# A decoder mixer layer on one core: weight-block sums moved and spread, linear attention's sums on another engine, and an extra turn for background steps

## The chip, the cores and the metric

The kernel runs on one core of a Trainium2 chip. The time is the device time of one execution in microseconds, as the median of several runs. In the profile PE is TensorE (PEld its weight loads), DVE is VectorE, ACT is ScalarE, POOL is GpSimd and SP is SyncE, whose queue here issues loads.

## The reference

One layer, 256 tokens, width 2048, all in float32. Two causal token mixers run side by side on one projection, are gated, merged and projected out:

```python
h = rmsnorm(x, pre_norm_g[l])
proj = h @ w_in[l]
(a_q, a_k, a_v, a_g, a_lr, b_q, b_k, b_v, b_g, m_a, m_b) = jnp.split(proj, offsets, axis=-1)
gk = jax.nn.log_sigmoid((a_lr @ gla_gk_w2[l] + gla_gk_b[l])) / GATE_LOGIT_NORMALIZER
o_a = gla_chunked(a_q, a_k, a_v, gk)            # 4 heads, keys 256, values 512, chunks of 64
o_a = rmsnorm(o_a, gla_norm_g[l]) * jax.nn.silu(a_g)
y_a = o_a @ w_branch_a[l]
o_b = diff_attention(b_q, b_k, b_v, lam)        # 16 heads, two softmaxes of 64 each, values 128
o_b = rmsnorm(o_b, diff_norm_g[l]) * (1.0 - lam_init) * jax.nn.silu(b_g)
y_b = o_b @ w_branch_b[l]
merged = jax.nn.sigmoid(m_a) * y_a + jax.nn.sigmoid(m_b) * y_b
x = x + rmsnorm(merged @ w_out[l], post_norm_g[l])
```

In `gla_chunked` the score of a query t and a key s is the sum over the key's elements of q, k and exp(b_t - b_s), where b is the running sum of the gate; in `diff_attention` the weights are one softmax minus lam times another.

## The kernel before

**Weights.** All weight matrices lie in one DRAM array in the order in which they are used. They are taken in halves of 128 x 1024 elements. `emit_half` loads a half (SP's queue), makes a rounded part `hi` of it on ScalarE (L244) and the rest `lo` on VectorE (L245); each product is then three matmuls: hi with both parts of the other operand, lo with the first part. `take` keeps four halves emitted ahead of the one in use (`AHEAD`); `hi` and `lo` have three buffers each. A token-major half (`half_tile`, L421) is 12 matmuls of up to 512 columns, a channel-major half (`half_channel`, L441 and L443) 8 of 512 and 8 of 256.

**Sets.** Five "sets" of weight blocks are multiplied by seven products instead of eight (`block_products`, L706), in the order 1, 3, 5, 6, 2, 7, 4. Each product has a left operand that is a sum of blocks. Per set and block row t = 0, 1 there are two running tiles, `a` and `b`, and a raw block. Product 1 takes `a`; then a DMA on POOL's queue adds a further block to `a` (L201). Product 3 takes `b`, product 5 takes `a`, product 6 takes a + b, product 2 the raw block, product 7 takes `b` after another accumulating DMA, and product 4 takes `a` plus the raw block. `emit_set` is called when a half is emitted, ahead of its split, and `follow_set` just behind the split. Products 1, 6, 7 and 4 accumulate in one PSUM bank `x`; between them VectorE or ScalarE reads it (L711, L717, L724). The set halves (six matmuls each) alternate with halves of other projections by the fixed order of `phase_steps`.

**Background work.** After the sets come token-major and channel-major projections: `ag0` to `ag3`, `m01`, the heads of groups 0 and 1, `m02`, `y00` to `y03` (branch a), the heads of groups 2 and 3, `m03`, `y10` to `y13` (branch b) and `o0` to `o3`. Under them run generators in the list `tasks`: `forget_gate`, `gla_scores` (one for each half of the four linear-attention heads), `gla_out`, and `diff_pair` (one for each two heads of a group of four). `pump(n)` gives one turn to each of the first n tasks: it runs them to their next `yield`. In token-major products it comes after every second half (after every half until the gate is done), in channel-major products after both halves of a channel. A task that yields after its last step is taken off the list by one more turn. A `diff_pair` makes for each of its two heads: scores (L933, L934) with the softmax's exponentials (L944), the combination (L951), transposes (L955), values (L963 to L965) with the norm (L969 to L976), and at the end transposes of both heads (L981). A group's pairs start when both pairs of the group before are done. `settle`, called in `y10` ahead of half 6, runs all tasks to their end.

**Linear attention's scores.** `gla_scores` fetches q and k from DRAM by POOL's queue, multiplies them on POOL (L769), adds channel pairs on POOL (L767), and in the first of seven levels does the same with a product shifted by one token (L785, L767). The results are split (L787 on ScalarE, L788 on VectorE).

**Order.** Instructions are listed in program order and then ordered for each engine by a planner with its own estimates of cost; an instruction may be placed earlier than its turn when its inputs and buffers are there. `issue_after` keeps TensorE's part of a turn behind the half last multiplied. Each engine runs its queue in that order and stands still at an instruction whose inputs are missing.

Of the kernel before, what the change touches and what calls it, by code (L numbers as in the profile page):

```python
# [91 lines left out]
def hybrid_kernel(ctx: ExitStack, tc, xt, xn, preg, postg, w, w2, gkb, glag, lamv, diffg, ident_d, causal_d, lmask_d, out):  # L92
# [84 lines left out]
    def emit_set(s, prod, t, h):  # L177
        c = slice(1024 * h, 1024 * h + 1024)
        if h == 0 and prod == 1:
            if s == 0:  # L180
                link(s, "a", t)
            link(s, "b", t)
        if h == 0 and prod == 4 and s + 1 < SETS:
            link(s + 1, "a", t)
        n = 4 * PRODUCTS.index(prod) + 2 * t + h + LEAD - 4 * PRODUCTS.index(2)
        if 0 <= n < 4:
            i, j = n // 2, n % 2
            raws[s, i, j] = u([P, 1024], "c")
            sp.dma_start(raws[s, i, j], weights(f"set{s}", 4 + i)[0][:, 1024 * j : 1024 * j + 1024])
        a, b = chain[s, "a", t], chain[s, "b", t]  # L190
        if prod == 6:
            dve.tensor_tensor(out=a[:, c], in0=a[:, c], in1=b[:, c], op=ALU.add)
        return raws[s, t, h] if prod == 2 else (b if prod in (3, 7) else a)[:, c]

    def follow_set(s, prod, t, h):
        c = slice(1024 * h, 1024 * h + 1024)
        a, b = chain[s, "a", t], chain[s, "b", t]
        if prod == 2:
            dve.tensor_tensor(out=a[:, c], in0=a[:, c], in1=raws[s, t, h], op=ALU.add)
        if h == 1 and prod in (1, 6):  # L200
            pool.dma_start(a if prod == 1 else b, weights(f"set{s}", 2 + t)[0], accum_op=ALU.add)  # L201

    def emit_plain(j, key, r, h):
        src, size = weights(key, r)
# [173 lines left out]
    done = set()  # L378
    latest = [None]

    def pump(n=1):
        with tc.issue_after(latest[0]):
            for task in tasks[:n]:
                if next(task, DONE) is DONE:
                    tasks.remove(task)

    def product(out, pairs, first, last):
        for n, (lhs, rhs) in enumerate(pairs):
# [35 lines left out]
    def token_major(key, n, ops, step=1, settle=None):  # L424
        banks = [ps("mm"), ps("mm")]
        for q in range(KT // 2):
            if q == 6 and settle:
                settle()
            half_tile(banks, n, q, ops, *take(key))
            if q % 2 or "gate" not in done:  # L430
                pump(step)
        return banks

    def half_channel(o, h, hi, lo):
# [11 lines left out]
    def channel_major(key):  # L446
        o = ps("mm")
        for h in range(2):
            half_channel(o, h, *take(key))
        return o[:, :S], o[:, S:]  # L450

    def gate(bank, b, dst):
# [297 lines left out]
    def gla_scores(hf):  # L750
        q, k = (fetch(ts[name, hf], name, u) for name in ("q", "k"))
        while "gate" not in done:
            yield
        pre = gp[hf]
        suf = u2([P, 2, 4, P], "suf")
        aall = u2([P, 3, 2, P], "att")
        a = aall[:, :2]
        ah, al = u2([P, 3, 2, P], "ath", F32R), u2([P, 3, 2, P], "atl", F32R)
        att[hf] = ah, al
        flat3 = "p a h t -> p (a h t)"  # L760
        es, eh, el = aall.rearrange(flat3), ah.rearrange(flat3), al.rearrange(flat3)
        pairs = "p (g i t) -> p g i t"

        def add_pairs(dst, src, n):
            dst = dst.rearrange("p (g t) -> p g t", t=n)
            src = src.rearrange(pairs, i=2, t=n)
            pool.tensor_tensor(out=dst, in0=src[:, :, 0, :], in1=src[:, :, 1, :], op=ALU.add)  # L767

        pool.tensor_tensor(out=suf, in0=q, in1=k, op=ALU.mult)  # L769
        add_pairs(es[:, :512], suf.rearrange("p b c t -> p (b c t)"), P)  # L770
        pool.memset(suf, 0.0)
        yield
        for n, m in enumerate(LEVELS):
            segs = 256 // m
            late = ((512 - m, 2), (2 * m, segs), (1, m))
            early = ((512 + m, 2), (2 * m, segs), (1, m))
            xq = t2([P, 512], "xq")
            xqv = xq.rearrange("p (b s m) -> p b s m", b=2, m=m)
            if m > 1:
                xk = t2([P, 512], "xk")  # L780
                xkv = view(xk, 0, (m, 2), (2 * m, segs), (1, m))
            act.activation(xqv, view(pre, m, *late), AF.Exp, scale=1.0 / 16.0)
            dve.tensor_tensor(out=xqv, in0=xqv, in1=view(q, m, *late), op=ALU.mult)
            if m == 1:
                pool.tensor_tensor(out=xqv, in0=xqv, in1=view(k, 0, *early), op=ALU.mult)  # L785
                add_pairs(es[:, 512:], xq, 64)
                act.activation(eh, es, AF.Copy)  # L787
                dve.tensor_tensor(out=el, in0=es, in1=f32(eh), op=ALU.subtract)  # L788
                pool.memset(a, 0.0)
            else:  # L790
                act.activation(xkv, view(suf, 0, *early), AF.Exp, scale=1.0 / 16.0)
                dve.tensor_tensor(out=xkv, in0=xkv, in1=view(k, 0, *early), op=ALU.mult)
            dve.tensor_tensor(out=view(suf, 0, *early), in0=view(suf, 0, *early), in1=view(pre, 2 * m - 1, (513 - 2 * m, 2), (2 * m, segs), (0, m)), op=ALU.add)
            dve.tensor_tensor(out=view(pre, m, *late), in0=view(pre, m, *late), in1=view(pre, m - 1, (513, 2), (2 * m, segs), (0, m)), op=ALU.add)
            yield
            bank = ps("bg")
            if m == 1:
                yield
                full = ps("bg")
                for o, c in ((full, slice(0, 512)), (bank[:, :S], slice(512, 768))):  # L800
                    pe.matmul(o, ones_r, eh[:, c], start=True, stop=False)
                    pe.matmul(o, ones_r, el[:, c], start=False, stop=True)
                dve.copy_predicated(a.rearrange("p b h t -> p (b h t)"), lmask[:, 7:9, :].rearrange("p a t -> p (a t)"), full)
            else:
                for h in range(2):
                    o = bank[:, :S].rearrange("p (b h t) -> p b h t", b=2, h=2)[:, :, h, :]
                    for i in range(2):
                        c = 2 * h + i
                        pe.matmul(o, xk[:, P * c : P * c + P], xq.rearrange("p (b c t) -> p b c t", b=2, c=4)[:, :, c, :], start=i == 0, stop=i == 1)
            dims = ((256 - m, 2), (2 * m, P // m), (1, m))  # L810
            dve.copy_predicated(view(aall, m, *dims), lmask[:, n, :].rearrange("p (b s m) -> p b s m", b=2, m=m), bank[:, :S].rearrange("p (b s m) -> p b s m", b=2, m=m))
            yield
        xq = t2([P, 512], "xq")
        xk = t2([P, 512], "xk")
        flat = "p c t -> p (c t)"
        act.activation(xq, pre[:, 1].rearrange(flat), AF.Exp, scale=1.0 / 16.0)
        dve.tensor_tensor(out=xq, in0=xq, in1=q[:, 1].rearrange(flat), op=ALU.mult)
        act.activation(xk, suf[:, 0].rearrange(flat), AF.Exp, scale=1.0 / 16.0)
        dve.tensor_tensor(out=xk, in0=xk, in1=k[:, 0].rearrange(flat), op=ALU.mult)
        yield  # L820
        bank = ps("bg")
        for h in range(2):
            for i in range(2):
                c = slice(P * (2 * h + i), P * (2 * h + i) + P)
                pe.matmul(bank[:, P * h : P * h + P], xk[:, c], xq[:, c], start=i == 0, stop=i == 1)
        act.activation(aall[:, 2].rearrange(flat), bank[:, :S], AF.Copy)
        act.activation(ah, aall, AF.Copy)
        dve.tensor_tensor(out=al, in0=aall, in1=f32(ah), op=ALU.subtract)
        done.add(f"scores{hf}")
        yield  # L830

    for hf in range(2):
        tasks.append(gla_scores(hf))
# [4 lines left out]
    def gla_out(hf, gates):  # L838
# [27 lines left out]
        for j in range(4):  # L866
            bank = ps("bg")
            for h in range(2):
                for b in range(2):
                    pe.transpose(bank[:, P * (2 * h + b) : P * (2 * h + b) + P], og[h][:, b, P * j : P * j + P], ident)  # L870
            i = 2 * hf + j // 2
            hi = oah[i][:, j % 2].rearrange("p h t -> p (h t)")
            lo = oal[i][:, j % 2].rearrange("p h t -> p (h t)")
            split_out(bank, hi, lo, glag_s[:, j : j + 1])
            if j % 2:
                yield
        done.add(f"out{hf}")

# [28 lines left out]
    def diff_pair(g, pair, values):  # L907
# [15 lines left out]
        for h in (2 * pair, 2 * pair + 1):  # L923
# [50 lines left out]
            dve.tensor_tensor(out=e, in0=e, in1=half_rstd, op=ALU.mult)  # L974
            for b in range(2):
                dve.scalar_tensor_tensor(out=og[:, h % 2, b, :], in0=bank[:, P * b : P * b + P], scalar=e[:, b : b + 1], in1=uu[:, b, hv], op0=ALU.mult, op1=ALU.mult)  # L976
            yield
        bank = ps("bg")
        for i in range(2):
            for b in range(2):  # L980
# [2 lines left out]
        lo = ol[:, 2 * pair : 2 * pair + 2, :].rearrange("p h t -> p (h t)")  # L983
        split_out(bank, hi, lo, diffg_s)
        done.add(f"pair{g}{pair}")
        yield

    def diff_heads(g):
        values = []
# [228 lines left out]
```

## Time and profile before

| | |
|---|---|
| median of 3 runs | 1121.78 us (1121.51 to 1122.82) |
| the profiled execution's own time | 1123.6 us |
| its span, first to last instruction | 1121.8 us |
| granted TensorE clock, mean | 0.997 |
| TensorE busy | 1105.6 us |
| VectorE, ScalarE, POOL busy | 831.8, 677.1, 111.8 us |

The lines of the profile give start and length in us, engine, source line and operation, the tile written and those read. In brackets stands how long the engine had been idle before, and what ended that. A matmul's end is modelled: a shown length overlaps with the next start.

### The profile page before, as it was taken

The numbers are of one execution on the slowest core, as the hardware profiler recorded it, in microseconds if no ns is written. First come the engines' busy times: TensorE is split into PE (matmuls) and PEld (weight loads), VectorE is DVE, ScalarE is ACT, GpSimd is POOL, SyncE is SP. The second block draws the span as 40 slices with busy tenths as digits, with TensorE's granted clock in tenths as the row PEclk, the third lists the DMA queues.
The fourth block names the chain that finished last, engine by engine and source line by source line (L and its number), as shares of the span: only waits on it lengthen the run. The fifth ranks groups of instructions, "written<-read, shape, count | busy, mean of one in ns | idle before, by whom it ended". The sixth has DMA issues, their size and how long they took to land. (4 is left out here: it accounts for less than half of the span.)

```text
span 1121.8 us, 15070 instructions
## 1 busy us (share of the span) xinstructions
PE 1105.6 (99%) x5570; PEld 945.4 (84%) x5570; DVE 831.8 (74%) x1160; ACT 677.1 (60%) x997; POOL 111.8 (10%) x165
## 2 busy tenths in 40 slices
PE   9999999999999999999999999999999999999996
PEld 7998888888888888878888888788888888788886
DVE  7878979779789798699965866766676766655463
ACT  7856666666666666765655755655675665444450
POOL 0101010000100100340021202111200010000000
PEclk9999999999999999999999999999999999999998
DMA  8799797696996973945586567565645474556752
GB/s 313 261 412 243 260 321 221 221 304 188 336 254 218 313 210 123 317 167 185 174 291 243 200 220 257 202 228 176 237 165 184 158 308 161 180 188 218 269 188 75
DMA packets 46042, 257.76 MB, mean 230 GB/s; under 512 B 5841, under 2 KB 7377, under 8 KB 23441
## 3 DMA queue, kind: packets, MB, share of 16 engines
q1 hardware_dynamic: 31968, 198.59, 49.4%
q0 software_dynamic: 12992, 56.89, 18.1%
q10 hardware_dynamic: 1008, 1.32, 0.4%
q8 instruction: 43, 0.70, 0.2%
q14 instruction: 31, 0.25, 0.1%
HBM read 236.86 MB, written 19.92 MB: 229 GB/s over the span
## 5 line engine op out<-in xcount | busy, mean ns | idle before, releaser
L245 DVE TENSOR_TENSOR lo<-raw,hi 128x1024 fp32r<-128x1024 f32 (+3 forms) x307 | 369.1, 1205 | 183.8 <-ACT hi L244 180.8
L244 ACT ACTIVATE hi<-raw 128x1024 fp32r<-128x1024 f32 (+3 forms) x307 | 315.8, 1032 | 282.0 <-PE mm L421 144.6
L421 PE MATMUL mm<-hi,xs 128*128 128x512 f32 (+1 forms) x704 | 171.4, 385 | 0.0
L421 PEld LDWEIGHTS mm<-hi,xs 128*128 128x128 f32 x704 | 130.2, 188 | 21.2
L245 DVE TENSOR_TENSOR lo<-a,hi 128x1024 fp32r<-128x1024 f32 x80 | 97.2, 1221 | 19.0 <-ACT hi L244 18.0
L244 ACT ACTIVATE hi<-a 128x1024 fp32r<-128x1024 f32 x80 | 84.7, 1059 | 39.4 <-PE mm L706 20.0
L441 PE MATMUL mm<-xs,hi 128*128 128x512 f32 x384 | 100.5, 396 | 0.0
L441 PE MATMUL bg<-xs,hi 128*128 128x512 f32 x384 | 99.5, 390 | 0.2 <-ACT hi L244 0.2
L421 PE MATMUL mm<-lo,xs 128*128 128x512 f32 (+1 forms) x352 | 91.9, 383 | 0.7 <-DVE lo L245 0.7
L441 PEld LDWEIGHTS bg<-xs,hi 128*128 128x128 f32 x384 | 72.1, 188 | 14.7 <-ACT hi L244 0.6
L441 PEld LDWEIGHTS mm<-xs,hi 128*128 128x128 f32 x384 | 69.2, 189 | 11.8
L421 PEld LDWEIGHTS mm<-lo,xs 128*128 128x128 f32 x352 | 65.8, 188 | 12.9 <-DVE lo L245 1.6
L706 PE MATMUL mm<-hi,xs 128*128 128x512 f32 x240 | 65.1, 393 | 0.8 <-DVE gr L724 0.8
L443 PEld LDWEIGHTS bg<-xs,lo 128*128 128x128 f32 x384 | 52.3, 190 | 4.9 <-DVE lo L245 1.2
L443 PEld LDWEIGHTS mm<-xs,lo 128*128 128x128 f32 x384 | 52.4, 190 | 3.8
L245 DVE TENSOR_TENSOR lo<-b,hi 128x1024 fp32r<-128x1024 f32 x40 | 48.6, 1221 | 8.5 <-ACT hi L244 7.8
L443 PE MATMUL bg<-xs,lo 128*128 128x256 f32 x384 | 53.6, 282 | 0.8 <-DVE lo L245 0.8
L443 PE MATMUL mm<-xs,lo 128*128 128x256 f32 x384 | 53.5, 282 | 0.0
L706 PEld LDWEIGHTS mm<-hi,xs 128*128 128x128 f32 x240 | 44.4, 188 | 9.7 <-DVE gr L724 1.5
L421 PE MATMUL mm<-hi,oah 128*128 128x512 f32 x128 | 50.7, 396 | 0.0
L421 PE MATMUL mm<-hi,obh 128*128 128x512 f32 x128 | 50.7, 399 | 0.0
L421 PE MATMUL mm<-hi,obl 128*128 128x512 f32 x128 | 50.1, 392 | 0.0
(301 smaller groups left out, 1966.6 us busy)
## 6 DMA issues: line engine op xcount, KB each, us to landing
raw<-in_w_dram SPq DMA_DIRECT2D x136, 1024.0 KB, 5.0
raw<-in_w_dram SPq DMA_DIRECT2D x14, 832.0 KB, 6.0
a<-in_w_dram SPq DMA_DIRECT2D x10, 1024.0 KB, 6.3
b<-in_w_dram SPq DMA_DIRECT2D x10, 1024.0 KB, 7.4
c<-in_w_dram SPq DMA_DIRECT2D x20, 512.0 KB, 10.3
a<-in_w_dram POOLq DMA_DIRECT2D x10, 1024.0 KB, 15.1
b<-in_w_dram POOLq DMA_DIRECT2D x10, 1024.0 KB, 9.5
raw<-in_w_dram SPq DMA_DIRECT2D x4, 800.0 KB, 9.7
```

What stands on the lines that cost most here:

```text
L244: act.activation(hi_t[:, a:b], r[:, a:b], AF.Copy)
L245: dve.tensor_tensor(out=lo_t[:, a:b], in0=r[:, a:b], in1=f32(hi_t[:, a:b]), op=ALU.subtract)
L421: i = pe.matmul(banks[b][:, :n], a[part][:, P * b : P * b + P], w[:, n * j : n * j + n], start=first, stop=last)
L441: i = pe.matmul(o, hi[:, c], x_pair(kt), start=kt == 0, stop=kt == KT - 1)
L443: i = pe.matmul(o[:, :S], lo[:, c], x_ops(kt)[0], start=False, stop=False)
L706: i = pe.matmul(out, a[part], w[:, 512 * j : 512 * j + 512], start=first, stop=last, skip_group_check=out is x)
```

## The change

There are three parts. First, the additions a + b and a + raw on VectorE: for block row 0 they are issued behind the halves of the second block row of the product before (product 5, product 2), for block row 1 behind the halves of the first block row of the product itself (product 6) or the next (product 7). The accumulating DMA into `b` follows behind them. Second, four elementwise operations of `gla_scores` go from POOL to VectorE. Third, the `yield` behind the last step of `gla_scores`, `gla_out` and `diff_pair` is gone, and a `diff_pair` whose first head is finished yields "go"; such a task gets a turn after the half at which no pump is due as well.

```diff
-        if prod == 6:
-            dve.tensor_tensor(out=a[:, c], in0=a[:, c], in1=b[:, c], op=ALU.add)
...
-        if prod == 2:
-            dve.tensor_tensor(out=a[:, c], in0=a[:, c], in1=raws[s, t, h], op=ALU.add)
-        if h == 1 and prod in (1, 6):
-            pool.dma_start(a if prod == 1 else b, weights(f"set{s}", 2 + t)[0], accum_op=ALU.add)
+
+        def accumulate(name, i):
+            pool.dma_start(chain[s, name, i], weights(f"set{s}", 2 + i)[0], accum_op=ALU.add)
+
+        if prod == 1 and h == 1:
+            accumulate("a", t)
+        i = {(5, 1): 0, (6, 0): 1, (2, 1): 0, (7, 0): 1}.get((prod, t))
+        if i is not None:
+            a = chain[s, "a", i][:, c]
+            second = prod in (5, 6)
+            dve.tensor_tensor(out=a, in0=a, in1=chain[s, "b", i][:, c] if second else raws[s, i, h], op=ALU.add)
+            if second and h == 1:
+                accumulate("b", i)
...
+    eager = set()
+
+    def advance(some):
+        with tc.issue_after(latest[0]):
+            for task in some:
+                r = next(task, DONE)
+                (eager.add if r == "go" else eager.discard)(task)
+                if r is DONE:
+                    tasks.remove(task)
+
     def pump(n=1):
-        with tc.issue_after(latest[0]):
-            for task in tasks[:n]:
-                if next(task, DONE) is DONE:
-                    tasks.remove(task)
+        advance(tasks[:n])
+
+    def pump_eager():
+        advance([task for task in tasks[:2] if task in eager])
...
             if q % 2 or "gate" not in done:
                 pump(step)
+            else:
+                pump_eager()
...
             half_channel(o, h, *take(key))
+            if h == 0:
+                pump_eager()
...
-            pool.tensor_tensor(out=dst, in0=src[:, :, 0, :], in1=src[:, :, 1, :], op=ALU.add)
-
-        pool.tensor_tensor(out=suf, in0=q, in1=k, op=ALU.mult)
+            dve.tensor_tensor(out=dst, in0=src[:, :, 0, :], in1=src[:, :, 1, :], op=ALU.add)
+
+        dve.tensor_tensor(out=suf, in0=q, in1=k, op=ALU.mult)
...
-                pool.tensor_tensor(out=xqv, in0=xqv, in1=view(k, 0, *early), op=ALU.mult)
+                dve.tensor_tensor(out=xqv, in0=xqv, in1=view(k, 0, *early), op=ALU.mult)
...
         done.add(f"scores{hf}")
-        yield
...
-            if j % 2:
+            if j == 1:
                 yield
...
-            yield
+            yield "go" if h % 2 == 0 else None
...
         done.add(f"pair{g}{pair}")
-        yield
```

More of the change, by code (lines that the diff above doesn't have):

```diff
@@ L196, in follow_set @@
         c = slice(1024 * h, 1024 * h + 1024)
-        a, b = chain[s, "a", t], chain[s, "b", t]
-        if prod == 2:
-            dve.tensor_tensor(out=a[:, c], in0=a[:, c], in1=raws[s, t, h], op=ALU.add)
-        if h == 1 and prod in (1, 6):
-            pool.dma_start(a if prod == 1 else b, weights(f"set{s}", 2 + t)[0], accum_op=ALU.add)
+        def accumulate(name, i):
[9 more added lines that the diff above has]
+                accumulate("b", i)
     def emit_plain(j, key, r, h):
```

## The prediction, before the result

> **What bounds the kernel now.** I read the page first: which engine is full.
>
> ```profile
> span 1121.8 us, 15070 instructions
> ...
> PE 1105.6 (99%) x5570; PEld 945.4 (84%) x5570; DVE 831.8 (74%) x1160; ACT 677.1 (60%) x997; POOL 111.8 (10%) x165
> ```
>
> TensorE is busy nearly from end to end, and nothing in the diff adds or removes a matmul. The change can only move the moments in which TensorE stands still. So the second view is what TensorE waited for. The two rows left out belong to the start of the program, before any edited line runs.
>
> ```profile
> PE bg L981 <- DVE ogb L976: 1.5, 2, 0.9
> PE bg L443 <- DVE lo L245: 0.8, 1, 0.8
> PE mm L706 <- DVE gr L724: 0.8, 2, 0.5
> PE mm L421 <- DVE lo L245: 0.7, 2, 0.5
> ...
> PE bg L955 <- DVE prob L951: 0.3, 1, 0.3
> PE bg L441 <- ACT hi L244: 0.2, 1, 0.2
> ```
>
> These are nine waits and 4.3 us. They are a little longer than shown, because a matmul's shown length is not its pace. The first row below is from the chain that ended last, the second from the instruction groups kept apart by shape:
>
> ```profile
> 972.68 16.35 PE mm L421 x72
> ...
> L421 PE MATMUL mm<-hi,obh 128*128 128x512 f32 x128 | 50.7, 399 | 0.0
> ```
>
> Seventy-two matmuls in a row take 16.35 us, 0.227 us each, while one alone is shown with about 0.39 us. A wait eats the overlap of about 0.17 us as well, so each costs its idle time plus 0.17: 4.3 + 9 x 0.17 = 5.8 us. That is the ceiling of any gain. One token-major half is 12 such matmuls, 2.73 us.
>
> The timeline of TensorE shows the nine places, with the idle time before each in brackets.
>
> ```profile
> 140.94 1.19 PE L706 MATMUL mm<-hi,xs 128*128 128x512 f32 x4 [0.51 <-DVE gr L724]
> 257.01 1.21 PE L443 MATMUL bg<-xs,lo 128*128 128x256 f32 x8 [0.81 <-DVE lo L245]
> 291.93 1.19 PE L706 MATMUL mm<-hi,xs 128*128 128x512 f32 x4 [0.26 <-DVE gr L724]
> 363.98 0.50 PE L441 MATMUL bg<-xs,hi 128*128 128x512 f32 x1 [0.20 <-ACT hi L244]
> 493.73 1.20 PE L421 MATMUL mm<-lo,xs 128*128 128x512 f32 x4 [0.49 <-DVE lo L245]
> 500.45 0.73 PE L421 MATMUL mm<-lo,xs 128*128 128x512 f32 x2 [0.25 <-DVE lo L245]
> 711.55 0.59 PE L981 MATMUL bg<-ident,ogb 128*128 128x128 f32 x2 [0.91 <-DVE ogb L976]
> 952.79 0.33 PE L955 MATMUL bg<-ident,prob 128*128 128x128 f32 x1 [0.26 <-DVE prob L951]
> 957.54 0.33 PE L981 MATMUL bg<-ident,ogb 128*128 128x128 f32 x1 [0.57 <-DVE ogb L976]
> ```
>
> **The change, part by part.** *Sums of weight blocks.* The four additions of product 6 stand in VectorE's queue in front of the splits that need them, and the four of product 2 follow at once. VectorE around the wait at 257.01:
>
> ```profile
> L192 DVE TENSOR_TENSOR a<-a,b 128x1024 f32<-128x1024 f32 x20 | 24.3, 1221 | 0.2
> ...
> 251.19 1.22 DVE L192 TENSOR_TENSOR a<-a,b 128x1024 f32<-128x1024 f32 x1
> ...
> 253.46 2.36 DVE L192 TENSOR_TENSOR a<-a,b 128x1024 f32<-128x1024 f32 x2
> 255.74 1.22 DVE L245 TENSOR_TENSOR lo<-raw,hi 128x1024 fp32r<-128x1024 f32 x1
> ```
>
> Three additions pass within 5 us, and the lo part at 255.74, and the next, come late. After the change there are still eight additions of 1.22 us a set, but four lie over the last two halves of product 5 and the first two of product 6, then come four halves without any, then four over products 2 and 7. A sum then stands two halves ahead of the split that reads it. Total VectorE work is the same; it hides under the matmuls of those halves, and where it didn't it would cost what 257.01 costs now. The wait there is worth 0.81 + 0.17 = 0.98 us; I take 0.9 of it. The accumulating DMA into b goes two halves earlier in POOL's queue, ahead only of spills, and its reader comes eight halves later: nothing. The waits at 140.94 and 291.93 (0.68 + 0.43) are another thing: product 4 accumulates in the bank that L724 has just to read, with no other half between them. The diff leaves that alone: 0. The one at 363.98 is 0.37; no edited line is named there: 0.
>
> *Linear attention's sums.* Four operations for each half of the heads leave POOL for VectorE:
>
> ```profile
> L769 POOL TENSOR_TENSOR suf<-q,k 128x1024 f32<-128x1024 f32 x2 | 5.3, 2664 | 6.6 <-DMA k<-k 6.6
> L767 POOL TENSOR_TENSOR att<-suf 128x512 f32<-128x512 f32 x2 | 4.0, 1980 | 0.1
> L785 POOL TENSOR_TENSOR xq<-xq,k 128x512 f32<-128x512 f32 x2 | 3.3, 1628 | 15.5 <-DVE xq L783 15.5
> L767 POOL TENSOR_TENSOR att<-xq 128x256 f32<-128x256 f32 x2 | 2.8, 1390 | 0.1
> ...
> L792 DVE TENSOR_TENSOR xk<-xk,k 128x512 f32<-128x512 f32 x12 | 8.3, 689 | 0.0
> ```
>
> On VectorE the 1024-wide product costs as L192, 1.22; the 512-wide ones as L792, 0.69 each; the last between nothing and 0.69, say 0.4. That is 3.0 us a half, 6.0 in all. Against that, VectorE's own work is stretched while POOL computes:
>
> ```profile
> 463.85 3.30 DVE L245 TENSOR_TENSOR lo<-raw,hi 128x1024 fp32r<-128x1024 f32 x1
> ...
> 483.43 0.70 DVE L783 TENSOR_TENSOR xq<-xq,q 128x512 f32<-128x512 f32 x1 [0.21 <-ACT xq L782]
> ...
> 487.66 2.90 DVE L783 TENSOR_TENSOR xq<-xq,q 128x512 f32<-128x512 f32 x1
> 491.36 2.32 DVE L245 TENSOR_TENSOR lo<-raw,hi 128x1024 fp32r<-128x1024 f32 x1
> ...
> 496.00 0.85 ACT L787 ACTIVATE ath<-att 128x768 fp32r<-128x768 f32 x1 [6.04 <-POOL att L767]
> ```
>
> The lo part takes 3.30 and 2.32 instead of 1.22, the product 2.90 instead of 0.70: 2.08 + 1.10 + 2.20 = 5.4 us given back by these three alone. So VectorE is about even, and what goes is the 6.04 us in which ScalarE stands at L787, with the weight splits queued behind it. POOL's DMA issues no longer stand behind these products; none of them is waited for there, so that is worth nothing. The two waits of TensorE at 493.73 and 500.45 sit in this stretch: 0.49 + 0.25 + 2 x 0.17 = 1.08; I take 1.0. If the additions didn't fit, they would cost at most these waits again.
>
> *Turns.* Counting the generators' turns by the code: a pair of heads took twelve turns of pump (ten where nothing is fetched), now ten (eight), plus one extra turn, half a step early, for the second head's scores. The pairs of groups 0 to 2 end one to five turns sooner, but under halves where TensorE isn't waiting for them. What counts is the end: the last pair's scores move from after half 5 of y10 to after half 4, 2.73 us earlier, and only three steps (transposes, values, final) are left for settle instead of four. The waits at 952.79 and 957.54, 0.26 + 0.57 + 0.34 = 1.17, lie on that chain and are shorter than 2.73; I take 0.9. The wait at 711.55 (0.91 + 0.17 = 1.08) is the second pair of group 0. Its distance to the step before stays one turn, and what delays it is ScalarE and VectorE work of the next group's split pulled in front of it, so between 0 and 1.08: I take half, 0.5.
>
> The extra turn's eight score matmuls need two free banks; the trace has no such turn. Its cost lies between zero and the longest wait of a background matmul now, 0.91 + 0.17. With re-planned order I allow 0.5 for all new waits.
>
> *Sum:* 0.9 + 1.0 + 0.9 + 0.5 - 0.5 = 2.8 us less. The profiled execution took 1123.6 us (span 1121.8 and 1.8 around it), 1.8 above the median of 1121.78. 1123.6 - 2.8 = 1120.8, and on the scale of the median **1119.0**. About 0.2% (2.2 us) is what a measurement of this kernel can tell, so faster begins below 1119.5. This case's own range is 1116.4 (nearly all 5.8) to 1120.6.
>
> A rule against this reading: the Trainium skill, Perfetto Trace Analysis, "Identifying the Most-Contended Engine", says that matmul busy time is no measure of how close TensorE is to its limit, and that the busy share of weight loads is. The page's row has 84% there, so by the rule TensorE would have room; the 72 matmuls at one pace speak against it in this kernel.
>
> **The rivals.** *A, slower: the product q·k at the head of VectorE's queue waits for its DMA.* On POOL this wait harmed nobody. Rows of the timelines, the waits and the tile k:
>
> ```profile
> POOL suf L769 <- DMA k<-k: 6.6, 1, 6.6
> ...
> 462.60 1.22 DVE L490 TENSOR_TENSOR w_s<-w_raw,w2h 64x1024 fp32r<-64x1024 f32 x1 [0.86 <-ACT w2h L489]
> ...
> 463.92 1.19 PE L499 MATMUL bg<-lrt,w_s 128*128 128x256 f32 x8
> ...
> L131 POOL DMA_DIRECT2D k<-k x2: 537/557/577, 453.2 to 456.5; - x2
> ...
> DMA to landing us min/median/max: 10.3/11.7/13.1
> ```
>
> k arrives at 453.2 + 10.3 = 463.5, the other half's at 456.5 + 13.1 = 469.6. If the planner puts q·k and its pair sum into the gap of 0.86 us before L490, they hold VectorE until 463.5 + 1.22 + 0.69 = 465.4; L490 starts 2.8 us late, and L499 on TensorE, which follows 0.1 us behind it now, as late. The second half, behind L490 and one lo part (465.4 + 2 x 1.22 = 467.8), would wait 1.8 and take 1.9: another 3.7. That makes 6.5: 1119.0 + 6.5 = 1125.5. It decides for slower from 5.0 us on (2.8 + 2.2). Against it: on POOL the second product ran at 487, long after its data. For it: POOL idled 6.6 us on the first.
>
> *B, no change: the waits move.* A background step in front of a planned slot makes another late, as ScalarE's `q` copies did at 711. If the terms 0.9 and 0.5 of the turns come back as new waits, 1.4 is left: 1123.6 - 1.4 - 1.8 = 1120.4.
>
> *C: TensorE isn't the bound, the splits are.* Then the 20 additions that stand before a split (24.3 us at L192) would come out whole: 1123.6 - 24.3 - 1.8 = 1097.5. The even pace of the 72 matmuls speaks against it. This is what the rule above would give.
>
> **How the numbers follow.** Forecast 0.60, of which 0.06 fall short of 2.2 us; B 0.24; A 0.14; C 0.02. Faster 0.54 + 0.02 = 0.56; same 0.06 + 0.24 = 0.30; slower 0.14. The range reaches from the forecast's lower end, 1116.4, past B into the first half of A (one product waits: 1119.0 + 2.8 and a lo part of 1.22): 1123.0.
>
> **What would show it.** Right: no wait of TensorE near the old 257 and 493 us; no POOL tensor_tensor but the small powers, lo parts at 1.22 throughout 460 to 500, and ScalarE's L787 no longer waiting for POOL; the last scores one half earlier and the waits before the last transposes gone; the L724 waits still there. Wrong: a row of VectorE waiting for the DMA of k, TensorE waiting for L490's result, or new waits at score matmuls for a bank. A span shorter by over 6 us would mean that the bound was not TensorE.

## The result, and the profile after

The changed kernel takes 1126.34 us (median of 5 runs, 1126.11 to 1127.47). The kernel before took 1122.5 us beside it (5 runs). The ratio is 1.0032, with a 95% interval of 1.0020 to 1.0044: 0.3% slower, with the whole interval above 1, where 1119.0 was forecast, and above the range (1116.4 to 1123.0).

The page of the changed kernel:

```profile
span 1124.6 us, 15079 instructions
...
PE 1107.0 (98%) x5570; PEld 948.3 (84%) x5570; DVE 828.6 (74%) x1168; ACT 679.2 (60%) x997; POOL 94.9 (8%) x157
```

The span grew by 2.8 us (1121.8 before), with as many matmuls. POOL lost 16.9 us of busy time, and VectorE, which took POOL's work over, is not busier (828.6 against 831.8). The waits of TensorE (total, times, longest):

```profile
PE bg L952 <- DVE ogb L995: 2.8, 1, 2.8
PE bg L1000 <- DVE ogb L995: 1.7, 2, 1.1
...
PE mm L726 <- DVE gr L744: 0.8, 2, 0.5
...
PE bg L974 <- DVE prob L970: 0.3, 1, 0.3
PE bg L459 <- ACT hi L250: 0.2, 1, 0.2
```

The two rows of waits for `lo` (three waits, 1.5 us) are gone. L1000, L726, L974 and L459 are the old L981, L706, L955 and L441, and these waits stayed. The first row is new. TensorE's timeline shows where:

```profile
692.30 0.33 PE L1000 MATMUL bg<-ident,ogb 128*128 128x128 f32 x1 [1.06 <-DVE ogb L995]
...
813.15 0.39 PE L984 MATMUL bg<-dv,wt 128*128 128x128 f32 x2
...
816.14 0.22 PE L952 MATMUL bg<-kh,q 128*128 128x128 f32 x1
...
819.81 0.22 PE L952 MATMUL bg<-kh,q 128*128 128x128 f32 x1
819.87 0.28 PE L953 MATMUL bg<-kl,q 128*128 128x128 f32 x1
822.91 0.44 PE L952 MATMUL bg<-kh,q 128*128 128x128 f32 x1 [2.76 <-DVE ogb L995]
...
824.33 3.62 PE L437 MATMUL mm<-hi,xs 128*128 128x512 f32 x8
827.74 1.77 PE L437 MATMUL mm<-lo,xs 128*128 128x512 f32 x4
829.36 2.00 PE L437 MATMUL mm<-hi,xs 128*128 128x512 f32 x8
...
945.72 0.22 PE L952 MATMUL bg<-kh,q 128*128 128x128 f32 x1
...
952.84 0.30 PE L974 MATMUL bg<-ident,prob 128*128 128x128 f32 x1 [0.34 <-DVE prob L970]
957.57 0.33 PE L1000 MATMUL bg<-ident,ogb 128*128 128x128 f32 x1 [0.64 <-DVE ogb L995]
```

At 819.81 the scores of the second pair of group 2 begin in one PSUM bank. They need a second bank, and the four tagged `bg` are then all in use: this one, one with the first pair's values (L984, 813.15), and two with the scores of its second head, which got the extra turn (816.14). The next to come free is the value bank, when L995 has read it. Without the wait 822.91 would have followed 819.87 after some 0.11 us, so the stop costs 2.93 us.

Behind it the matmuls are slow. The half that begins at 824.33 takes 5.0 us to the next at 829.36; a half is 2.73. The windows of the trace (length, five engines, then the granted clock) show why:

```profile
815.50:822.40 6.90, 4.65 (x26) 3.89 (x24) 3.10 (x6) 4.42 (x9) 0.71 (x1) 1.00 0.14 57
822.40:829.20 6.80, 6.29 (x18) 5.26 (x19) 5.17 (x22) 3.96 (x10) 0.00 (x0) 0.50 0.46 154
829.20:836.00 6.80, 6.80 (x33) 5.59 (x32) 4.71 (x14) 5.82 (x14) 0.00 (x0) 1.00 0.47 157
```

After the stop the granted clock is 0.50 for 6.8 us. Taken against the pace at full clock, the matmuls of this stretch come about 3.0 us late. So the loss in this execution is 2.93 + 3.0 = 5.9 us; the starts that were late before and are not now give back 3.1 us, and 5.9 - 3.1 = 2.8 is the growth of the span.

The Trainium skill, TensorE: Matmul & The Clock Gate, "Part 1: The HAM clock gate", states that the clock falls to half after about one window of 3.4 us idle, that the window runs freely and that full clock needs some 3.4 us of work. The trace agrees on the half and on the length (6.8 us is two such windows), but 2.76 us idle was enough here.

Why was the value bank late? ScalarE's timeline after, then before:

```profile
817.82 0.63 ACT L919 ACTIVATE kh<-dk 64x512 fp32r<-64x512 f32 x1 [2.42 <-DMA dk<-dk]
818.48 0.63 ACT L920 ACTIVATE kh<-dk 64x512 fp32r<-64x512 f32 x1
819.13 0.28 ACT L988 ACTIVATE junkd<-bg 128x128 bf16<-128x128 f32 x1
...
820.17 0.28 ACT L988 ACTIVATE junkd<-bg 128x128 bf16<-128x128 f32 x1
```

```profile
814.89 0.63 ACT L900 ACTIVATE kh<-dk 64x512 fp32r<-64x512 f32 x1 [0.94 <-DMA dk<-dk]
...
822.26 0.28 ACT L969 ACTIVATE junkd<-bg 128x128 bf16<-128x128 f32 x1 [0.51 <-PE bg L965]
```

The squares of the values (L988, before L969) start the norm that ends in L995. Before, they ran right behind their matmuls, long after the split of the other pair's `dk`. Now the values are ready at 813.5, but the squares are queued behind that split, and ScalarE stands there for a DMA. `dk` is spilled to DRAM and fetched back at once. POOL's issues, first before, then after:

```profile
807.45 0.55 POOL L126 DMA_DIRECT2D dk<-dk  x1 [9.52 <-DVE dk L619]
...
810.32 0.54 POOL L131 DMA_DIRECT2D dk<-dk  x1 [1.79 <-PE mm L421]
...
DMA to landing us min/median/max: 2.3/3.4/4.5
```

```profile
807.29 0.54 POOL L126 DMA_DIRECT2D dk<-dk  x1 [13.14 <-DVE dk L639]
...
812.96 0.54 POOL L131 DMA_DIRECT2D dk<-dk  x1 [4.58 <-DMA dk<-dk]
...
DMA to landing us min/median/max: 4.8/5.0/5.1
```

Each line of landing times holds the spill and its fetch. The fetch goes out behind the landing of the spill, which took 5.1 us instead of 2.3; so the fetch was issued 2.6 us later (812.96 against 810.32) and `dk` arrived 2.9 us later (817.82 against 814.89). So two things met: values that come earlier, and a `dk` that comes later.

### The profile page after: what moved, and what is told of

It reads as the page before. It is cut to its first block, busy times and chain, and to the rows that moved or that the text cites. A ratio compares the mean times of both kernels' runs of the same rounds, so it can differ in the third digit from the quotient of the medians.

```text
span 1124.6 us, 15079 instructions
## 1 busy us (share of the span) xinstructions
PE 1107.0 (98%) x5570; PEld 948.3 (84%) x5570; DVE 828.6 (74%) x1168; ACT 679.2 (60%) x997; POOL 94.9 (8%) x157
## 3 DMA queue, kind: packets, MB, share of 16 engines
q0 software_dynamic: 12992, 56.89, 18.1%
## 4 chain that ended last, share of the span: by engine, by line
PE 82%; issue 10%; DMA 2%; ACT 2%; DVE 2%; POOL 1%; POOLq 0%; DVEq 0%; SPq 0%; ACTq 0%
PE mm L437 34%; PE mm L726 17%; PE bg L459 7%; PE mm L459 5%; PE bg L461 4%; PE bg L437 3%; PE mm L461 2%; DMA dk<-dk 2%; PE bg L420 2%; PE mm L405 2%; PE mm L420 2%; PE bg L829 1%; PE bg L405 1%; ACT hi L250 1%; DVE lo L251 1%
## 5 line engine op out<-in xcount | busy, mean ns | idle before, releaser
L251 DVE TENSOR_TENSOR lo<-raw,hi 128x1024 fp32r<-128x1024 f32 (+3 forms) x307 | 365.1, 1191 | 189.6 <-ACT hi L250 178.5
L459 PE MATMUL bg<-xs,hi 128*128 128x512 f32 x384 | 99.4, 390 | 0.2 <-ACT hi L250 0.2
L459 PE MATMUL mm<-xs,hi 128*128 128x512 f32 x384 | 99.5, 395 | 0.0
L459 PEld LDWEIGHTS bg<-xs,hi 128*128 128x128 f32 x384 | 72.1, 188 | 14.6 <-ACT hi L250 0.6
L459 PEld LDWEIGHTS mm<-xs,hi 128*128 128x128 f32 x384 | 69.2, 189 | 11.9
L726 PE MATMUL mm<-hi,xs 128*128 128x512 f32 x240 | 65.1, 393 | 0.8 <-DVE gr L744 0.8
L726 PEld LDWEIGHTS mm<-hi,xs 128*128 128x128 f32 x240 | 44.4, 188 | 9.7 <-DVE gr L744 1.5
L250 ACT ACTIVATE hi<-b 128x1024 fp32r<-128x1024 f32 x40 | 42.4, 1060 | 13.3 <-PE mm L726 9.0
```

What stands on the lines that cost most here:

```text
L250: act.activation(hi_t[:, a:b], r[:, a:b], AF.Copy)
L251: dve.tensor_tensor(out=lo_t[:, a:b], in0=r[:, a:b], in1=f32(hi_t[:, a:b]), op=ALU.subtract)
L459: i = pe.matmul(o, hi[:, c], x_pair(kt), start=kt == 0, stop=kt == KT - 1)
L726: i = pe.matmul(out, a[part], w[:, 512 * j : 512 * j + 512], start=first, stop=last, skip_group_check=out is x)
```

## The experiments

Each time is a median of 11 or 12 runs (5 for the third part alone). "Before" is the kernel before, run beside it on the same chip; a ratio is against that, and can differ from the quotient of the two medians by up to 0.1%.

**Without the extra turn** (1125.08 us, before 1123.14; ratio 1.0025, 1.0010 to 1.0040).

```diff
...
-                pump_eager()
+                pass
...
-                pump_eager()
+                pass
...
```

> The changed kernel without the extra turn (pump_eager is never called); the removed yields and both other parts stay. Theory: TensorE stands 2.9 us in group 2 because the second score bank of the second pair is still held by the first pair's values, and the halved clock behind it costs 3.0 us more. Without the extra turn the two pairs' scores come one behind the other in the same place, so four banks are wanted at once and the fourth is still not free: a shorter wait of about 1.9 us at L952 near 821 us, the clock perhaps whole. Then 1.0 us (clock still halved) to 4.0 us (clock whole) below the changed kernel, 0 to 3 us above the kernel before. Rival (the extra turn by itself is the whole cost): no wait at L952, and the gains of the other parts are left, about 3 us below the kernel before.

```profile
823.12 0.30 PE L952 MATMUL bg<-kh,q 128*128 128x128 f32 x1 [2.17 <-DVE ogb L995]
```

The wait stays, 2.17 us, and the clock falls for 3.4 us. The time is 0.0007 of the ratio, 0.8 us, below the changed kernel's, where 1.0 to 4.0 was expected, and the intervals overlap. So it isn't the extra turn's own scores that cost the time; that the pairs end a turn sooner is enough to bring them together.

**The wait filled with matmuls** (1125.27, before 1123.14; 1.0024, 1.0015 to 1.0033). Twenty-six matmuls write columns of the score bank that nobody reads, where TensorE stood still.

```diff
+ [pe.matmul(banks[0][:, 3 * P :], q2[:, 0, i2, t], kh[:, 0, i2, :P], start=True, stop=True)
+   for _ in range(26 if (g, h, b, m) == (2, 2, 0, 0) else 0)]
```

> The changed kernel with 26 matmuls of 128 columns (2.9 us) added in front of the wait, into columns of the score bank that nobody reads; the output is unchanged. Theory (the idle time of TensorE is what halves the clock): the wait at L952 shrinks to under 0.3 us, the granted clock stays 1.0 and the 3.0 us that the matmuls behind it lost come back: about 0.5 us above the kernel before. Rival (the clock falls there for another reason, or costs nothing): clock 0.5 for some us again and the time stays 3 to 4 us above the kernel before.

```profile
821.03 3.07 PE L953 MATMUL bg<-kh,q 128*128 128x128 f32 x26
...
836.59 0.49 PE L982 MATMUL bg<-dv,wt 128*128 128x128 f32 x2 [0.44 <-ACT wt L976]
```

With the fill in place the granted clock stayed at 1.00 in this profile, as it would if idle time is what lowers it. One profile doesn't show that, because the changed kernel too has a profile in which the clock stays whole at this stop (below). In time the case is not made: 0.5 us above the kernel before was expected, and 2.7 came by the ratio. The gain on the changed kernel is 0.0008 of the ratio or 0.9 us, with intervals that overlap. A new wait at 836.59 took some of it. So the 3.0 us are what the profiled execution lost; as a mean over runs they aren't shown.

**`dk` and `dq` of that pair kept in SBUF** (1122.67, before 1123.14; 0.9996, 0.9988 to 1.0004). No spill and no fetch for pair (2, 1).

```diff
-            tq, tk = (fetch(heads[g, pair, name], name, ...) for name in ("dq", "dk"))
+            tq, tk = (heads[g, pair, name] if (g, pair) == (2, 1) else fetch(...) for name in ("dq", "dk"))
...
-                    heads[g, pair, name] = spill(t, name)
+                    heads[g, pair, name] = t if (g, pair) == (2, 1) else spill(t, name)
```

> The changed kernel, but the second pair's dq and dk of group 2 stay in SBUF instead of being spilled to DRAM and fetched back; turns, banks and all else as changed. Theory (ScalarE stands at L919 for the DMA that brings dk back, the squares L988 are queued behind it, so the value bank comes free late): no wait of ScalarE for dk's DMA, squares about 3 us earlier, no wait of TensorE at L952, clock whole: about 6 us below the changed kernel, 2.5 us below the kernel before. Rival (too few banks whatever ScalarE does, because the extra turn comes half a step early): TensorE still waits 2 us or more at L952 and the time is within 1 us of the changed kernel.

Neither the wait at the scores nor a fall of the clock is left, and the time is 0.0036 of the ratio, 4 us, below the changed kernel's (6 expected). With no DMA ahead of it the split doesn't hold the squares up. This version is still 0.0017 of the ratio, 1.9 us, above the next one, so the meeting of the two pairs is not the whole price of its turns; where some of the rest lies is shown at the end of this section.

**First and second part, turns as before** (1121.04, before 1123.14; 0.9979, 0.9971 to 0.9988).

Against the changed kernel the turns go back to what they were:

```diff
...
-                pump_eager()
+                pass
...
-            if j == 1:
+            if j % 2:
...
-        done.add(f"pair{g}{pair}")
+        done.add(f"pair{g}{pair}"); yield
```

> The first two parts of the change alone: block sums spread, linear attention's sums on VectorE; turns as in the kernel before. Theory (these two parts did what they should: the waits near 126, 257, 493 and 500 us are gone, worth 3.1 us by the starts of the matmuls): 3 us below the kernel before (1.6 to 3.6). Rival (part of the loss is theirs): less than 1 us below, or above it.

By the ratio this is faster than the kernel before by 2.4 us, and the waits at 257, 493 and 500 are gone in it. The loss comes with the third part.

**The third part alone, on the kernel before** (1129.18, before 1124.18; 1.0035, 1.0022 to 1.0048).

```diff
...
             half_tile(banks, n, q, ops, *take(key))
             if q % 2 or "gate" not in done:
                 pump(step)
+            else:
+                pump_eager()
...
-            yield
+            yield "go" if h % 2 == 0 else None
...
         done.add(f"pair{g}{pair}")
-        yield
```

> The third part alone on the kernel before: extra turn and removed yields; sums and POOL work as before. Theory: the loss in group 2 is all of the third part's, so the time is that of the changed kernel plus the 2.1 us that the other two parts were worth: 5 to 6 us above the kernel before, with the wait at L952 (here at its own line) and the halved clock. Rival (the loss needs the parts together): less than 3 us above.

```profile
827.44 0.45 PE L946 MATMUL bg<-kh,q 128*128 128x128 f32 x1 [2.29 <-DVE ogb L989]
```

The wait comes without the first two parts too, and half clock of 3.4 us with it. The loss is 3.9 us by the ratio (2.5 to 5.4), where 5 to 6 was expected and less than 3 by the rival; these five runs don't decide between theory and rival.

**The extra turn, with the old ends** (1126.35, before 1124.18; 1.0016, 1.0005 to 1.0027). The three `yield`s behind the last steps are put back.

```diff
-        done.add(f"pair{g}{pair}")
+        done.add(f"pair{g}{pair}"); yield
```

> The changed kernel with the three yields at the ends put back; the extra turn stays. Theory (what hurts is that the first pair of group 2 comes one turn earlier against the spill and fetch of the second pair, by whichever means): the extra turns of groups 0 and 1 move it as far as the removed yields did, so the order on TensorE in group 2 is that of the changed kernel, the wait of 2 to 3 us at L952 and the halved clock come back, and the time is within 1.5 us of the changed kernel. Rival (the removed yields are the cause, the extra turn is harmless): no such wait, about 2 us below the kernel before, as with the first two parts alone.

```profile
825.79 0.45 PE L952 MATMUL bg<-kh,q 128*128 128x128 f32 x1 [3.30 <-DVE ogb L995]
```

The wait is there, and longer. Either way of saving a turn makes the pairs meet.

**Group 2's first pair one turn later** (1121.85, before 1124.18; 0.9980, 0.9971 to 0.9990). All three parts stay; only this pair idles for one turn ahead of its split.

```diff
-            yield
+            yield from (None,) * (2 if (g, pair) == (2, 0) else 1)
```

> The changed kernel with one idle turn put in front of the first split of group 2, so that this pair stands against the second pair's spill and fetch as in the kernel before; extra turns and removed yields stay. Theory (the meeting of the two is the whole of the loss): no wait of TensorE over 0.5 us between 800 and 830, clock whole, about 2 us below the kernel before, 5 to 6 below the changed kernel. Rival (the extra turn costs in every group, through banks or crowded engines): 1 us or more above the first two parts alone (which were 2.1 below the kernel before).

Beside it in the same hour the changed kernel ran again:

> The changed kernel itself, on the chip and in the hour of the three others, for direct comparison: 3.6 us above the kernel before (2 to 5), with the wait at L952 and the halved clock behind it.

It took 1126.65 us (1.0028, 1.0016 to 1.0040). So one turn less of haste is worth 4.8 us, nearly the whole loss of the third part (5.5 us between the ratios of the changed kernel here and of the first two parts alone, 1.0028 and 0.9979). In the changed kernel's second profile TensorE waited 2.26 us at L952 for the same reason, but the clock there stayed whole:

```profile
820.00:826.00 6.00, 3.74 (x21) 3.13 (x21) 3.76 (x10) 4.02 (x9) 0.71 (x1) 1.00 0.00 0
```

**The parts one by one, and both good versions again.** The kernel before took 1122.89 us beside these four. The first part alone, on the kernel before:

```diff
...
-        if prod == 6:
-            dve.tensor_tensor(out=a[:, c], in0=a[:, c], in1=b[:, c], op=ALU.add)
...
+        i = {(5, 1): 0, (6, 0): 1, (2, 1): 0, (7, 0): 1}.get((prod, t))
...
```

> The first part alone (the spread sums of weight blocks) on the kernel before. By the theory (the three parts act each in its own place, and the loss belongs to the turns): TensorE's wait at 257 is gone and nothing else moves, about 0.9 to 1.0 us below before, ratio 0.9991; the two waits near 493 and 500 stay, and no wait for ogb near 823. Rival (the sums alone shift the order enough to bring the pairs of group 2 together): above before, with an idle time of 2 us or more at the score matmuls near 823.

The second part alone:

```diff
...
-        pool.tensor_tensor(out=suf, in0=q, in1=k, op=ALU.mult)
+        dve.tensor_tensor(out=suf, in0=q, in1=k, op=ALU.mult)
...
```

> The second part alone (linear attention's four operations on VectorE) on the kernel before. By the theory: the waits at 493 and 500 are gone, the one at 257 stays, POOL shows no tensor_tensor of 512 or 1024 elements, about 1.0 to 1.1 us below before, ratio 0.9990. Rival (the prediction's case A: VectorE waits for the DMA of k): 2 to 6 us above before, with TensorE waiting near 463.

The two versions of above:

> First and second part together, turns as before, once more, beside the two parts alone and beside the next kernel. If the parts add up: 2.1 us below before (0.9979 to 0.9983), the sum of the two runs of single parts within 0.5 us.

> All three parts with group 2's first pair one turn later, once more, beside the first two parts alone. It tells what the turns are worth when group 2 is out of the way. By the prediction's term for the end of the kernel (0.9) and for the wait at 711 (0.5) it would be 0.9 to 1.4 us below the two parts alone; by what the trace of the changed kernel shows (both waits stayed) it is within 0.5 us of it.

| kernel | median, us | ratio | 95% interval |
|---|---|---|---|
| first part alone | 1122.44 | 0.9994 | 0.9986 to 1.0002 |
| second part alone | 1120.80 | 0.9985 | 0.9976 to 0.9993 |
| both, turns as before | 1121.20 | 0.9985 | 0.9975 to 0.9994 |
| all three, group 2 one turn later | 1122.02 | 0.9993 | 0.9983 to 1.0002 |

The two parts together are 1.7 us below the kernel before, where their single values add up to 2.4; the difference lies inside the intervals. Two results went clearly against what was expected. The wait at 257, which the first part was to remove, is gone with the second part alone, and then the first adds nothing that shows. VectorE's order there, with the second part alone, is that of before:

```profile
248.87 1.22 DVE L192 TENSOR_TENSOR a<-a,b 128x1024 f32<-128x1024 f32 x1
...
251.14 2.35 DVE L192 TENSOR_TENSOR a<-a,b 128x1024 f32<-128x1024 f32 x2
253.41 1.22 DVE L245 TENSOR_TENSOR lo<-raw,hi 128x1024 fp32r<-128x1024 f32 x1
```

It is one addition, a split, two additions, the split that TensorE waited for: so it stands in the kernel before, in the changed one and in each of the first two parts alone. The planner had already placed the additions so, and the new text moved some others by a few places. What differs is when the block sum arrives that POOL's DMA accumulates. The DMA's issue and the split of its result, before, and then in the third part alone:

```profile
230.87 0.89 POOL L201 DMA_DIRECT2D a<-in_w_dram  x1 [3.69 <-DVE lo L245]
248.96 2.01 ACT L244 ACTIVATE hi<-a 128x1024 fp32r<-128x1024 f32 x2 [2.71 <-PE mm L706]
```

```profile
232.87 0.89 POOL L201 DMA_DIRECT2D a<-in_w_dram  x1 [3.69 <-DVE lo L245]
250.71 2.01 ACT L244 ACTIVATE hi<-a 128x1024 fp32r<-128x1024 f32 x2 [2.46 <-DMA a<-in_w_dram]
```

That is 18.1 and 17.8 us, and both profiles have the wait. (The row of before names a matmul, but its DMA landed 18.0 us behind the issue, at 248.87.) In all others the split starts between 16.2 and 17.4 us behind the issue, and none has it. For example, the first part alone:

```profile
230.93 0.89 POOL L197 DMA_DIRECT2D a<-in_w_dram  x1 [3.69 <-DVE lo L251]
248.32 2.01 ACT L250 ACTIVATE hi<-a 128x1024 fp32r<-128x1024 f32 x2 [2.01 <-DMA a<-in_w_dram]
```

So the wait goes with a DMA that lands late in some executions; the additions lie between this split and the one that TensorE waits for, with and without the edit. Whether the first part makes the late landing rarer (it issues the sums into `b` earlier) isn't settled. Of three profiles without it two are late, of eleven with it none, which speaks for it; the time of the part alone can't be told from no change.

The other miss is the version with all three parts and group 2 delayed. It has no score wait, and still is 0.8 us above the first two parts alone; in the earlier comparisons the two had equal ratios (0.9980, 0.9979). Its profile shows a place where it loses. TensorE waits twice for the transposes of one pair:

```profile
695.06 0.33 PE L1000 MATMUL bg<-ident,ogb 128*128 128x128 f32 x1 [0.34 <-DVE ogb L995]
...
696.46 0.33 PE L1000 MATMUL bg<-ident,ogb 128*128 128x128 f32 x1 [1.07 <-DVE ogb L995]
```

The first two parts alone, in their second run, wait there once, 0.84 us at 710.38. From there to the end this version stands four times for `ogb` or `prob`, 2.38 us in all, and the first two parts three times, 1.68; with the overlap of 0.17 for the fourth wait that is 0.9 us. The kernel with `dk` and `dq` in SBUF has four such waits too, 2.71 us, which by the same count is 1.2 of its 1.9. No experiment took these waits out. The turns gain nothing where group 2 is out of the way, and the second part, with or without the first, is the best version found.

## Why the prediction was wrong

**The step that failed** is "With re-planned order I allow 0.5 for all new waits", bounded by "the longest wait of a background matmul now, 0.91 + 0.17". The place was named rightly (score matmuls that need two free banks, and a new wait there as a sign of being wrong), but the size came from a wait of another kind. In the trace of before the longest wait was one for work already under way. The new one is for a bank whose release stands in ScalarE's queue behind a DMA, and has no reason to stay near 1 us. In the profiled execution it took 2.93 us, and 3.0 more by the clock, which the sum didn't have at all: 5.9 instead of 0.5. The row to look at was ScalarE's 0.94 us for `dk` at 814.89. It showed a queue that stops for a round trip through DRAM, and the question was which instructions the earlier turns would put behind it.

**Turns, the end of the kernel:** 0.9 was forecast, 0 came. The last scores did come half a y10 earlier, at 945.72 in a kernel that runs 2.8 us behind, where they stood at 945.75. But the planner moved the transposes with them. In both kernels 25 matmuls stand between the last scores and the first transpose, so the waits at 952.84 and 957.57 remained, 0.51 + 0.80 against 0.42 + 0.74 (start to start). What was late was the distance between steps, which nobody changed; the start of the chain had been moved.

**Turns, the wait at 711:** 0.5 forecast. It is now at 692.30 with 1.06 us where it was 0.91. Nothing was gained.

**Second part:** 1.0 forecast; TensorE's waits at 493.73 and 500.45 are gone, and the part alone gives 0.9985 or 1.7 us (0.8 to 2.7). The prices on VectorE were right:

```profile
473.21 1.22 DVE L789 TENSOR_TENSOR suf<-q,k 128x1024 f32<-128x1024 f32 x1
...
476.08 0.68 DVE L787 TENSOR_TENSOR att<-suf 128x512 f32<-128x512 f32 x1
...
484.00 0.68 DVE L805 TENSOR_TENSOR xq<-xq,k 128x512 f32<-128x512 f32 x1
...
486.34 0.42 DVE L787 TENSOR_TENSOR att<-xq 128x256 f32<-128x256 f32 x1
```

They sum to 3.0 us a half, and VectorE's own work gave more than that back: with 6.0 us of added work its total fell from 831.8 to 828.6.

**First part:** 0.9 forecast, on the reading that the additions held the split up. The wait went in the profile, but around it the additions stand where they stood, the wait follows the landing of a DMA, and the part alone can't be told from nothing. That the term came true in the changed kernel's profile may be luck; it didn't show that the edit had done it.

**Rivals.** A did not come: the product q·k ran at 473, long after its data. It held all of the chance of slower, so that chance was given to something that didn't happen. B, the waits move, is the nearest, with the price far too low: it took back the turns' 1.4 but had no term for a new place of waiting. C did not come: nothing near 24 us was gained.

## What to carry to other kernels

Before a background step is moved earlier, list what will stand ahead of it on each in-order queue that it uses; if that is an instruction that waits for a DMA, every buffer the step holds is held for as long. An idle stretch of TensorE of some 2 us can bring half clock behind it, so its price is not the stretch alone. A wait that disappears in one profile is credited to an edit only when the queue order there has changed, and when several profiles without the edit have the wait and several with it don't.

## What had not been expected of the hardware

At the score matmuls of group 2, idle stretches of 2.17 to 3.30 us were followed by half clock of 3.4 us (without the extra turn; third part alone) or 6.8 us (changed kernel; extra turn with old ends), and once, after 2.26 us, by none. The changed kernel is in both, 6.8 us in one execution and none in another, so its loss to the clock varies from run to run. At the start of the program a stop for a weight split was followed by 3.4 us of half clock in four profiles (after 1.21, 1.61, 1.80 and 2.41 us idle: second run of the first two parts, second run of the changed kernel, second run of all three parts with group 2 one turn later, third part alone), and by none in others (1.53 us in the first run with group 2 one turn later; in that profile 2.01 us at 106.38 brought none either). So the length of a stop doesn't settle by itself whether the clock falls. The freely running window that the Trainium skill states (TensorE: Matmul & The Clock Gate, "Part 1: The HAM clock gate") could do that; the runs show no more than that the clock's answer varies.

The same 256 KB of `dk` from SBUF to DRAM landed in 2.3 us in one kernel and in 5.1 us in the other. The windows from 808 to 812, before and then after, show the DMA engines' share and GB/s in the last two columns:

```profile
808.00:812.00 4.00, 4.00 (x20) 3.30 (x19) 1.81 (x7) 2.70 (x9) 2.11 (x4) 1.00 0.80 244
```

```profile
808.00:812.00 4.00, 4.00 (x19) 3.32 (x18) 1.78 (x2) 1.06 (x1) 0.37 (x1) 1.00 0.97 348
```

After, the spill runs while a weight load has the engines full. That this load is what slows it is read from these rows; no experiment separated the two.
